# A gated delta net layer on one core: the order of instructions from a list instead of a list scheduler

## The chip, the cores and the metric

The kernel runs on one core of one Trainium2 chip. The metric is the device time of one launch in microseconds (us), and the kernel before takes 2705.01 us, the median of three runs (2702.5 to 2705.7). A core has TensorE (PE, matrix products), VectorE (DVE), ScalarE (ACT), GpSimd (POOL) and SyncE (SP, which issues transfers here). Each engine runs its own instructions in the order in which the program gives them, and waits on semaphores for the results of others.

## The reference, cut to what matters

One layer on 2048 tokens of width 1024: eight heads of a gated delta net (a linear attention with a state per head, in chunks) beside four heads of attention to a memory of 256 rows, an output projection, a layer norm, a squared-ReLU MLP of width 4096 and a second layer norm.

```python
proj = x @ w_in                                   # q, k, v, z, a, b and the memory queries
qkv = silu(causal_depthwise_conv(qkv, conv_w));  q, k = l2_normalize(q), l2_normalize(k)
beta = sigmoid(b);  g = -exp(a_log) * softplus(a + dt_bias)
# per chunk: A = I + strict_lower(beta k k^T * decay);  u, w = A^-1 (beta v), A^-1 (beta k e^g)
def step(state, inp):
    v_new = u_c - w_c @ state
    o = qd @ state + a_c @ v_new
    return state * dc + kd^T @ v_new, o
o = rms_norm(o, gate_norm_w) * silu(z)
m = memory_attention(mq, mem_k, mem_v)            # softmax over layer_norm(mem) @ w_mem_kv
x = layer_norm(ALPHA * x + concat(o, m) @ w_out, ln1_g, ln1_b)
x = layer_norm(ALPHA * x + square(relu(x @ w_ff1)) @ w_ff2, ln2_g, ln2_b)
```

## The kernel before, in words

Everything is float32. A large product is made of three passes of 128x512: each operand is split into a high part (a cast on ACT, `CAST whl<-wraw`, `CAST T<-xj`) and a low part (a subtraction on DVE), and `mm3` adds high x high, high x low and low x high. The tokens are worked in four blocks of 512.

*The mixer* goes through a block head by head. `dense` projects q, k and v (banks `aq`, `ak`, `av`), convolves them (`ck`, `cq`, `cv` are the results) and transposes them (`ptk`, `ptq`); `gate` projects z (`az`). `gdn_a` builds the matrix of a chunk (`pkq`), inverts it by a chain of small products with copies between them (`pq`, then `pp`, several times; the last copies, such as `Y<-pp` on ACT, write the inverse) and transposes v (`ptv`). `gdn_b` runs the recurrence (`pc`, `po`) and transposes the output (`pto`). The memory heads stand between (`amq`, `sps`, `pmT`, `pmo`); `memory_rows` makes the memory's keys and values ready once, beginning with sixteen transposes `pt<-ident,ym`, whose results ACT takes from the banks as `st`.

*The output projection* (`out_seven`, banks `ao`) and the two products of the MLP (`fA`, `fB`, `fC` and `f2A`, `f2B`, `f2C`) work on a pair of blocks by seven products in place of eight, with sums of operands kept in device memory. At the end of an output projection ACT normalises rows (`ACTIVATE y<-y,nb,rs`), PE transposes them (`pt<-ident,y`), ACT writes them out of the banks (`st<-pt,lnc`) and casts them (`CAST T<-st`), while the last of the seven products still runs; its weights come as `whl` (`CAST whl<-whl`).

*The start* (`first_tokens`): ten matmuls of ones (`warm`, two passes each), then the first 24 passes of `aq`, for which x comes in eight pieces (`xj`), with the sixteen products for a and b (`aab`) and a small transpose (`pln`) among them.

*What sets the order.* The code between the first constants and the end isn't issued as it is written. A `Recorder` keeps each operation with its reads and writes, and `issue` gives them all out at the end, so that all of them have one line in the profile, L447. In the kernel before, `issue` is a list scheduler: for each engine it keeps what is ready, takes what has the lowest priority number (an operation's index, plus `rec.shift`, plus an offset from the table `PLACE` of some 200 numbers that `spot` selects by stage), and adds up times by a table of costs (`cost`, `LAT`, `MARGIN`, `DRAIN`). It also models the number of buffers of a tag, so that no operation is given out before it has a place. `rec.gate` and `rec.join` hold transfers and matmuls behind others in this scheduler only. The program that results is run as usual: each engine in the order given, with the waits that reads and writes need.

Of the kernel before, what the change touches and what calls it, by code (L numbers as in the profile page):

```python
# [14 lines left out]
P = 128  # L15
# [14 lines left out]

LAT = {("PE", "PE"): 0, ("DVE", "POOL"): 190, ("ACT", "POOL"): 215, ("PE", "POOL"): 350, ("DVE", "DVE"): 130, ("ACT", "ACT"): 155, ("POOL", "POOL"): 100}
LAT_FROM = {"PE": 200, "DVE": 130, "ACT": 135, "POOL": 75, "SP": 60}
MARGIN, TURN = {"PE": 100, "DVE": 100, "ACT": 100, "POOL": 400, "SP": 100}, 40
DRAIN, SWITCH = {"DVE": 90, "ACT": 100, "POOL": 98}, 0


# [7 lines left out]
class Buf:  # L46


    def __init__(self, pool, shape, dtype, tag, bufs, name):
        self.pool, self.shape, self.dtype, self.tag, self.bufs, self.name = pool, shape, dtype, tag, bufs, name  # L50
        self.ap = None
        self.psum = pool.name == "ps"
        self.users = 0
        self.end = 0
        self.held = False
        self.first = None
        self.log = []
# [8 lines left out]

# [118 lines left out]
class Op:  # L185
    __slots__ = ("i", "eng", "fn", "args", "kw", "dur", "extra", "succ", "npred", "ready", "start", "end", "load", "last",
                 "bufs", "turns", "prio", "quads", "cols", "late", "lhs")


PLACE = {  # L190
# [31 lines left out]
}  # L222


class Recorder:
    def __init__(self, nc, tc):
        self.nc, self.tc, self.ops, self.shift, self.gate, self.base, self.join = nc, tc, [], 0, None, 0, []
        self.tags = {}
        for attr, eng in (("vector", "DVE"), ("scalar", "ACT"), ("gpsimd", "POOL"), ("tensor", "PE"), ("sync", "SP")):
            setattr(self, attr, _Engine(self, getattr(nc, attr), eng))  # L230

    def buf(self, pool, shape, dtype, tag, bufs, name):
        b = Buf(pool, shape, dtype, tag, bufs, name)
        self.tags.setdefault((pool.name, tag), []).append(b)
# [6 lines left out]
    def add(self, eng, fn, name, args, kw):  # L241
        o = Op()
        o.i, o.eng, o.fn, o.args, o.kw = len(self.ops), eng, fn, args, kw
        o.succ, o.npred, o.ready, o.extra, o.turns = [], 0, 0, 0, set()
        o.prio = o.i + self.shift + self.base
# [8 lines left out]
        o.dur = self.cost(o, name, wr, rd, args, kw)  # L254

        o.quads = {("r" if v in rd else "w", v.buf.psum): v.p0 // 32 for v in wr + rd[::-1]}
# [21 lines left out]
        for i, q in turns.items():  # L278
            if i not in preds:
                preds[i] = q  # L280
                q.turns.add(o.i)
        for q in preds.values():
            q.succ.append(o)
        o.npred = len(preds)
        o.bufs = list({id(r.buf): r.buf for r in rd + wr}.values())
        for b in o.bufs:
            if b.first is None:
                b.first = o.i
            b.users += 1
# [891 lines left out]

# [751 lines left out]
```

## Time and profile before

| | |
|---|---|
| median of three runs (lowest, highest) | 2705.01 us (2702.5, 2705.7) |
| profiled execution, its time | 2702.34 us |
| its span in the trace | 2700.6 us |
| PE busy | 2685.2 us, 99% |
| DVE, ACT, POOL busy | 2087.0 (77%), 1624.8 (60%), 423.3 us (16%) |
| share of the chain that ended last | PE 96%, DVE 2%, ACT 1% |
| transfers | 613.79 MB, 227 GB/s in the mean |

Busy time is the share of an engine's span in which the profile has an instruction on it. The ends of matmuls are modelled, and a matmul's recorded end lies behind the start of the next; distances between starts are the better measure of PE. The chain is followed back from the last instruction, at each step to what released it. In the timeline, a row is a run of instructions of one form: its start, the time from the first's start to the last's end, the engine, and behind `x` how many; in brackets the idle time before it and what ended it.

### The profile page before, as it was taken

The page shows a single profiled execution, that of the slowest core. Times are in us where ns is not written, and L with a number is a line of the kernel's source. Part 1 is how long each engine was busy: PE and PEld are TensorE (multiplying, and loading weights), DVE is VectorE, ACT ScalarE, POOL GpSimd, SP SyncE. Part 2 cuts the span into 40 slices and gives each one's busy share as a digit, 9 for nine tenths or more (in the row PEclk, how much of TensorE's full clock was granted, in tenths as well). Part 3 has the DMA queues.
Part 4 walks back from the last instruction along what each step waited for, and adds up shares of the span by engine and source line. Part 5 has one row for each costly group of instructions (what it writes and reads, how often), then busy time and mean ns, then how long its engine had stood idle before and what let it go on. Part 6 is the DMA issues. An engine that isn't in the chain of part 4 may idle for free.

```text
span 2700.6 us, 42393 instructions
## 1 busy us (share of the span) xinstructions
PE 2685.2 (99%) x13577; PEld 2248.5 (83%) x13577; DVE 2087.0 (77%) x5604; ACT 1624.8 (60%) x4098; POOL 423.3 (16%) x1023
## 2 busy tenths in 40 slices
PE   9999999999999999999999999999999999999998
PEld 7888888888888888888888888888887888888887
DVE  7998889998867776756778888789977656667575
ACT  7778777776575555334446776578756655544341
POOL 3333133331000000000032221233201000000001
PEclk9999999999999999999999999999999999999999
DMA  8676659868788888765664444444678644586673
GB/s 317 235 258 207 234 178 311 300 233 285 276 307 289 293 302 287 270 215 189 234 222 157 151 150 175 175 162 138 238 271 290 206 138 153 171 293 216 215 237 114
DMA packets 209070, 613.79 MB, mean 227 GB/s; under 512 B 24112, under 2 KB 32720, under 8 KB 188880
## 3 DMA queue, kind: packets, MB, share of 16 engines
q1 hardware_dynamic: 208416, 611.04, 65.0%
q8 instruction: 107, 1.75, 0.3%
q14 instruction: 115, 0.94, 0.1%
q10 hardware_dynamic: 432, 0.05, 0.0%
HBM read 436.35 MB, written 174.65 MB: 226 GB/s over the span
## 4 chain that ended last, share of the span: by engine, by line
PE 96%; DVE 2%; ACT 1%; DMA 0%; issue 0%; POOL 0%; POOLq 0%; ACTq 0%; DVEq 0%
PE f2A L447 13%; PE fA L447 13%; PE ao L447 8%; PE az L447 7%; PE fC L447 6%; PE f2C L447 6%; PE av L447 6%; PE ak L447 6%; PE aq L447 6%; PE fB L447 3%; PE f2B L447 3%; PE amq L447 3%; PE pc L447 3%; PE po L447 2%; PE pkq L447 2%; PE pq L447 1%
## 5 line engine op out<-in xcount | busy, mean ns | idle before, releaser
L447 DVE TENSOR_TENSOR whl<-wraw,whl 128x512 fp32r<-128x512 f32 (+2 forms) x294 | 256.9, 884 | 102.6 <-ACT whl L447 99.9
L447 ACT CAST whl<-wraw 128x512 fp32r<-128x512 f32 (+2 forms) x294 | 226.2, 780 | 182.6 <-PE fC L447 73.5
L447 PE MATMUL fA<-B,whl 128*128 128x512 f32 x1152 | 286.4, 389 | 0.0
L447 PE MATMUL f2A<-whl,X 128*128 128x512 f32 x1152 | 263.1, 389 | 0.0
L447 ACT CAST X<-X 128x1024 fp32r<-128x1024 f32 x118 | 124.1, 1052 | 228.1 <-DMA X<-xsc 174.6
L447 PEld LDWEIGHTS fA<-B,whl 128*128 128x128 f32 x1152 | 216.2, 188 | 45.0
L447 PEld LDWEIGHTS f2A<-whl,X 128*128 128x128 f32 x1152 | 216.3, 188 | 44.9
L447 DVE TENSOR_TENSOR X<-X,X 128x1024 fp32r<-128x1024 f32 x118 | 143.8, 1221 | 130.2 <-ACT X L447 130.0
L447 PE MATMUL az<-T,whl 128*128 128x512 f32 x768 | 215.9, 406 | 0.0
L447 PE MATMUL ak<-T,whl 128*128 128x512 f32 x768 | 213.4, 405 | 0.6 <-ACT cq L447 0.5
L447 PE MATMUL aq<-T,whl 128*128 128x512 f32 x768 | 210.6, 404 | 0.5 <-DVE T L447 0.4
L447 PE MATMUL av<-T,whl 128*128 128x512 f32 x768 | 209.3, 403 | 0.0
L447 PE MATMUL fC<-B,whl 128*128 128x512 f32 x768 | 196.9, 389 | 0.0
L447 PE MATMUL f2C<-whl,X 128*128 128x512 f32 x768 | 174.7, 389 | 0.0
L447 PEld LDWEIGHTS fC<-B,whl 128*128 128x128 f32 x768 | 144.1, 188 | 30.1 <-DVE B L447 0.2
L447 PEld LDWEIGHTS f2C<-whl,X 128*128 128x128 f32 x768 | 144.2, 188 | 29.9
L447 POOL TENSOR_SCALAR ve<-mv 128x1 f32<-128x1 f32 x34 | 15.6, 460 | 915.0 <-DVE mv L447 915.0
L447 PEld LDWEIGHTS aq<-T,whl 128*128 128x128 f32 x768 | 136.7, 189 | 25.3 <-DVE T L447 2.3
L447 PEld LDWEIGHTS ak<-T,whl 128*128 128x128 f32 x768 | 137.1, 189 | 24.3 <-ACT cq L447 0.6
L447 PEld LDWEIGHTS av<-T,whl 128*128 128x128 f32 x768 | 137.4, 189 | 23.2
L447 PEld LDWEIGHTS az<-T,whl 128*128 128x128 f32 x768 | 136.5, 189 | 22.4
L447 PE MATMUL ao<-whl,X 128*128 128x512 f32 x528 | 139.7, 403 | 0.0
(296 smaller groups left out, 6260.8 us busy)
## 6 DMA issues: line engine op xcount, KB each, us to landing
whl<-wsc SPq DMA_DIRECT2D x108, 1024.0 KB, 4.9
wraw<-in_w_ff_dram SPq DMA_DIRECT2D x106, 512.0 KB, 4.3
X<-xsc SPq DMA_DIRECT2D x96, 512.0 KB, 3.9
wsc<-whl SPq DMA_DIRECT2D x36, 1024.0 KB, 6.0
whl<-tsc SPq DMA_DIRECT2D x64, 512.0 KB, 4.8
xsc<-hB SPq DMA_DIRECT2D x96, 256.0 KB, 3.1
xo<-cat SPq DMA_DIRECT2D x80, 256.0 KB, 3.3
wraw<-in_w_in_dram SPq DMA_DIRECT2D x35, 512.0 KB, 5.9
```

The source lines that it names most:

```text
L447: o.fn(*[res(a) for a in o.args], **{k: res(v) for k, v in o.kw.items()})
```

## The change

The scheduler goes, with its costs, its offsets (`PLACE`, `spot`), shifts, gates and model of buffers. In its place stands a constant `ORDER`, a compressed and encoded string of some 260 lines, of which `order` makes the list of indices, each as the difference from the one before. `issue` takes the recorded operations in that order; it asserts that each comes behind those it depends on. The operations themselves, 23,656 of them, and their tiles are the same. In the profile their line is then L544.

```diff
-LAT = {("PE", "PE"): 0, ("DVE", "POOL"): 190, ("ACT", "POOL"): 215, ("PE", "POOL"): 350, ...}
-MARGIN, TURN = {"PE": 100, "DVE": 100, "ACT": 100, "POOL": 400, "SP": 100}, 40
...
-PLACE = {
-    ('w',): 140, (0, 0, 'D'): 5, (0, 0, 'F'): -5, (0, 0, 'H'): -585, (0, 1, 'D'): -70, (0, 1, 'F'): 75,
...
+    __slots__ = ("i", "eng", "fn", "args", "kw", "preds")
+ORDER = (
+    "c-rlKiIOC_j@%DLnDIXT|Hnjk2N;a3tezfeCGFa-&3j#0m6>rcNDy#19C2Rpy36`!*6W_@N8*q5$Jnp<@n5;xdUw6GzL49M`Esl`626eGQTVZY"
...
+def order():
+    import base64
+    import zlib
+
+    i = 0
+    for d in zlib.decompress(base64.b85decode(ORDER)).decode().split(","):
+        i += int(d)
+        yield i
...
-        o.prio = o.i + self.shift + self.base
...
-        if eng == "SP" and self.gate is not None:
-            preds[self.gate.i] = self.gate
-        if eng == "PE":
-            preds.update((q.i, q) for q in self.join)
...
+        o.preds = preds.keys() | turns.keys()
         self.ops.append(o)
...
     def issue(self):
-        import heapq
...
-            o = heapq.heappop(avail[e])[2]
...
-        out.sort(key=lambda o: (o.start, o.i))
+        out = [self.ops[i] for i in order()]
+        assert len({o.i for o in out}) == len(out) == len(self.ops)
+        done = set()
+        for o in out:
+            assert o.preds <= done, o.i
+            done.add(o.i)
         res = lambda v: v.get() if isinstance(v, Ref) else v
         with self.tc.manual_schedule():
             for o in out:
                 o.fn(*[res(a) for a in o.args], **{k: res(v) for k, v in o.kw.items()})
...
-    def spot(*key):
-        rec.base = PLACE.get(key, 0)
...
     def gate_rows(a, xs, ks):
-        rec.join = [q for x in xs for q, w, *_ in x.buf.log if w and q.eng == "SP"]
-        rec.shift -= 9999
```

Of PE's 12,495 recorded instructions 3,400 leave their relative order, of DVE's 5,089 1,862, of ACT's 3,648 1,468, of POOL's 1,014 485 and of SP's 1,410 482. PE's are moved by at most 214 places, in the median of those moved by 2. Three places follow.

PE at the start of the program, before; `warm` is the product of ones, `aq` the first projection, and the numbers behind `T` only tell tiles apart:

```order
L447 MATMUL warm<-ones 128x128 x10
L447 MATMUL aq<-T_157,whl 128x512
L447 MATMUL aq<-T_162,whl 128x512
L447 MATMUL aq<-T_157,whl 128x512 x2
L447 MATMUL aq<-T_162,whl 128x512
L447 MATMUL aq<-T_157,whl 128x512
L447 MATMUL aq<-T_176,whl 128x512
```

And in the list:

```order
L544 MATMUL aq<-T_104,whl 128x512
L544 MATMUL aq<-T_112,whl 128x512
L544 MATMUL warm<-ones 128x128 x10
L544 MATMUL aq<-T_104,whl 128x512 x2
L544 MATMUL aq<-T_112,whl 128x512
L544 MATMUL aq<-T_104,whl 128x512
L544 MATMUL aq<-T_138,whl 128x512
```

The products of ones, first before, now stand behind two passes of `aq`. On SP, the first transfer is now `xj` (before, a piece of `wraw`, then two of `xj`).

PE where the memory's rows are transposed, in the first block, before:

```order
L447 MATMUL az<-T_222,whl 128x512
L447 MATMUL az<-T_217,whl 128x512
L447 MATMUL pt<-ident,ym 128x128 x4
L447 MATMUL ptq<-ident,cq 128x128 x4
L447 MATMUL pt<-ident,ym 128x128 x12
L447 MATMUL aq<-T_157,whl 128x512
L447 MATMUL aq<-T_162,whl 128x512
```

And in the list, the first eight and, behind the `az`, the next:

```order
L544 MATMUL av<-T_202,whl 128x512
L544 MATMUL pkq<-kq 128x256
L544 MATMUL pt<-ident,ym 128x128 x8
L544 MATMUL ptk<-ident,ck 128x128 x4
L544 MATMUL az<-T_104,whl 128x512
L544 MATMUL az<-T_112,whl 128x512
L544 MATMUL az<-T_104,whl 128x512 x2
L544 MATMUL az<-T_112,whl 128x512
```

The sixteen transposes, four and twelve before, now stand as eight and, after some thirty rows, as 1, 1 and 6.

ACT near the end of the second output projection, where `y`, `st`, `T` and `whl` are as told above; before:

```order
L447 ACTIVATE y<-y,nb,rs 128x512
L447 ACTIVATE st<-pt,lnc 128x256 x2
L447 ACTIVATE y<-y,nb,rs 128x512
L447 CAST T_24186<-st 128x2x256
L447 ACTIVATE y<-y,nb,rs 128x512 x2
L447 CAST whl<-whl 128x1024 x2
L447 ACTIVATE st<-pt,lnc 128x256 x2
L447 CAST T_24226<-st 128x2x256
```

And in the list:

```order
L544 ACTIVATE y<-y,nb,rs 128x512
L544 CAST xh<-xl 128x512 x2
L544 ACTIVATE y<-y,nb,rs 128x512 x3
L544 ACTIVATE st<-pt,lnc 128x256 x2
L544 CAST whl<-whl 128x1024
L544 ACTIVATE st<-pt,lnc 128x256 x2
L544 CAST whl<-whl 128x1024
L544 CAST T_24204<-st 128x2x256
L544 CAST T_24206<-st 128x2x256
```

The four `y` stand in one piece of one and one of three, and the two casts of `whl`, together behind the last `y` before, now stand apart, each behind a pair of `st`. On PE, eleven transposes `pt<-ident,y` stood in one row there with `ao` behind them; now eight stand together, then 23 rows of `ao`, then nine. The last 14 rows of PE and of DVE in the program are the same in both.

## Rows read from the trace of the kernel before

**Rows 1.** The page, busy us, share of the span and instructions of each engine.

```profile
PE 2685.2 (99%) x13577; PEld 2248.5 (83%) x13577; DVE 2087.0 (77%) x5604; ACT 1624.8 (60%) x4098; POOL 423.3 (16%) x1023
```

**Rows 2.** The page, the chain that ended last, shares of the span.

```profile
PE 96%; DVE 2%; ACT 1%; DMA 0%; issue 0%; POOL 0%; POOLq 0%; ACTq 0%; DVEq 0%
```

**Rows 3.** Table of waits, PE: us in total, times, longest us.

```profile
PE ao L447 <- ACT whl L447: 1.4, 4, 0.6
...
PE pt L447 <- ACT st L447: 1.1, 1, 1.1
```

**Rows 4.** Busy us by stretch (PE, PEld, DVE, ACT, POOL), PEclk, DMA share, GB/s.

```profile
1.20:3.00 1.80, 1.80 (x8) 1.80 (x9) 0.56 (x2) 0.80 (x1) 1.76 (x7) 1.00 0.52 151
1146.00:1189.00 43.00, 43.00 (x191) 35.64 (x190) 26.46 (x29) 16.86 (x16) 2.10 (x4) 1.00 0.61 198
```

**Rows 5.** PE's timeline, end of the second output projection: start, us, line, operation.

```profile
2060.58 0.71 PE L447 MATMUL pt<-ident,y 128*128 128x128 f32 x5
2062.17 0.55 PE L447 MATMUL pt<-ident,y 128*128 128x128 f32 x3 [0.88 <-ACT y L447]
2062.88 0.55 PE L447 MATMUL pt<-ident,y 128*128 128x128 f32 x3 [0.16 <-ACT y L447]
2063.81 0.73 PE L447 MATMUL ao<-whl,xh 128*128 128x512 f32 x2 [0.39 <-ACT whl L447]
2064.76 0.96 PE L447 MATMUL ao<-whl,xh 128*128 128x512 f32 x3 [0.22 <-ACT whl L447]
```

**Rows 6.** ACT's timeline at the same place.

```profile
2062.72 1.99 ACT L447 CAST whl<-whl 128x1024 fp32r<-128x1024 f32 x2
```

**Rows 7.** PE's timeline, end of the first output projection.

```profile
733.20 0.27 PE L447 MATMUL pt<-ident,y 128*128 128x128 f32 x1
734.09 0.73 PE L447 MATMUL ao<-whl,xh 128*128 128x512 f32 x2 [0.62 <-ACT whl L447]
735.05 0.97 PE L447 MATMUL ao<-whl,xh 128*128 128x512 f32 x3 [0.22 <-ACT whl L447]
```

**Rows 8.** PE's timeline, the memory's rows.

```profile
53.02 0.82 PE L447 MATMUL pt<-ident,ym 128*128 128x128 f32 x6
54.95 0.66 PE L447 MATMUL pt<-ident,ym 128*128 128x128 f32 x4 [1.11 <-ACT st L447]
```

**Rows 9.** PE's timeline, `ak` behind `cq`.

```profile
507.81 1.88 PE L447 MATMUL ak<-T,whl 128*128 128x512 f32 x7 [0.49 <-ACT cq L447]
```

**Rows 10.** PE's timeline, small waits: the first, one of the largest, the last.

```profile
62.75 0.98 PE L447 MATMUL pkq<-kq 128*128 128x256 f32 x6
...
407.97 1.78 PE L447 MATMUL av<-T,whl 128*128 128x512 f32 x7
410.02 0.66 PE L447 MATMUL ptv<-ident,cv 128*128 128x128 f32 x4 [0.26 <-ACT Y L447]
...
1914.48 0.39 PE L447 MATMUL pc<-R,Y 128*128 128x128 f32 x2
```

**Rows 11.** PE's timeline, the start.

```profile
1.19 4.57 PE L447 MATMUL warm<-ones 128*128 128x128 f32 x20 [1.19 <-POOL mhalf L534]
5.48 0.51 PE L447 MATMUL aq<-T,whl 128*128 128x512 f32 x1
...
11.92 1.92 PE L447 MATMUL aab<-xj,abw 128*32 128x512 f32 x16
...
15.48 0.74 PE L447 MATMUL ak<-T,whl 128*128 128x512 f32 x2
```

**Rows 12.** SP's issues, the start.

```profile
0.79 0.39 SPq L447 DMA_DIRECT2D wraw<-in_w_in_dram  x1
1.24 0.90 SPq L447 DMA_DIRECT2D xj<-in_xt_dram  x2
```

**Rows 13.** ACT's timeline, the start.

```profile
4.79 0.62 ACT L447 CAST T<-xj 128x512 fp32r<-128x512 f32 x1 [0.80 <-DMA xj<-in_xt_dram]
```

**Rows 14.** PE's timeline, the last matmul.

```profile
2691.78 0.39 PE L447 MATMUL f2A<-whl,xl 128*128 128x512 f32 x1
```

More of the change, by code (lines that the diff above doesn't have):

```diff
@@ L27 @@
 QO, KO, VO, ZO, AO, MO = 0, 1024, 2048, 3072, 4096, 4112
-LAT = {("PE", "PE"): 0, ("DVE", "POOL"): 190, ("ACT", "POOL"): 215, ("PE", "POOL"): 350, ("DVE", "DVE"): 130, ("ACT", "ACT"): 155, ("POOL", "POOL"): 100}
-LAT_FROM = {"PE": 200, "DVE": 130, "ACT": 135, "POOL": 75, "SP": 60}
-MARGIN, TURN = {"PE": 100, "DVE": 100, "ACT": 100, "POOL": 400, "SP": 100}, 40
-DRAIN, SWITCH = {"DVE": 90, "ACT": 100, "POOL": 98}, 0
 def _prod(v):
@@ L52, in __init__ @@
         self.psum = pool.name == "ps"
[L53 to L56, printed above, removed]
         self.log = []
@@ L253, in add @@
         rd = [v for v in rd if isinstance(v, Ref)]
-        o.dur = self.cost(o, name, wr, rd, args, kw)
-        o.quads = {("r" if v in rd else "w", v.buf.psum): v.p0 // 32 for v in wr + rd[::-1]}
         preds, turns = {}, {}
@@ L336, in issue @@
-    def issue(self):
-        import heapq
-        engs = ("PE", "DVE", "ACT", "POOL", "SP")
-        free = {e: 0.0 for e in engs}
-        soon = {e: [] for e in engs}
-        avail = {e: [] for e in engs}
-        dma = [0.0]
-        quads, cols = {e: {} for e in DRAIN}, P
-        slots = {k: [0.0] * v[0].bufs for k, v in self.tags.items()}
-        order = {k: sorted((b for b in v if b.users), key=lambda b: b.first) for k, v in self.tags.items()}
-        pos = {}
-        for k, v in order.items():
-            for i, b in enumerate(v):
-                b.key = k
-        head = {k: 0 for k in order}
-        wait = {k: [] for k in order}
-        def ahead(b):
-            v, h = order[b.key], head[b.key]
-            while h < len(v) and v[h].held:
-                h += 1
-            head[b.key] = h
-            c = 0
-            while v[h] is not b:
-                c += not v[h].held
-                h += 1
-            return c
-        def place(o):
-            for b in o.bufs:
-                if not b.held:
-                    if len(slots[b.key]) <= ahead(b):
-                        wait[b.key].append(o)
-                        return
-                    b.held = True
-                    b.since = heapq.heappop(slots[b.key])
-                    again(b.key)
-                o.ready = max(o.ready, b.since)
-            heapq.heappush(soon[o.eng], (o.ready, o.i, o))
-        def again(k):
-            if wait[k]:
-                w, wait[k] = sorted(set(wait[k]), key=lambda q: q.i), []
-                for q in w:
-                    pending.append(q)
-        pending = [o for o in self.ops if o.npred == 0]
-        out = []
-        fed = 0.0
-        while True:
-            while pending:
-                place(pending.pop(0))
-            best = None
-            for e in engs:
-                if avail[e]:
-                    t = free[e]
-                elif soon[e]:
-                    t = max(free[e], soon[e][0][0])
-                else:
-                    continue
-                if best is None or t < best[0]:
-                    best = (t, e)
-            if best is None:
-                break
-            t, e = best
-            while soon[e] and soon[e][0][0] <= t:
-                r, i, o = heapq.heappop(soon[e])
-                heapq.heappush(avail[e], (o.prio, i, o))
-            o = heapq.heappop(avail[e])[2]
-            if e == "PE":
-                if o.cols != cols:
-                    t += SWITCH
-                    cols = o.cols
-                t = max(t, fed + o.load)
-                fed = t + o.dur - o.last
-            if e in DRAIN:
-                at = quads[e]
-                if any(at.get(k, q) != q for k, q in o.quads.items()):
-                    t = max(t, free[e] + DRAIN[e])
-                at.update(o.quads)
-            o.start, o.end = t, t + o.dur
-            free[e] = o.end
-            if o.extra:
-                dma[0] = max(o.end + 1700, dma[0]) + o.extra - 1700
-                o.end = dma[0] + o.late
-            out.append(o)
-            for s in o.succ:
-                lat = LAT.get((e, s.eng), LAT_FROM[e])
-                if e == "PE" and lat and o.last < 60:
-                    lat += 65 if o.last > 30 else 130
-                if lat:
-                    lat += MARGIN[e] + (s.load if s.eng == "PE" and s.lhs in o.bufs else 0)
-                s.ready = max(s.ready, o.end + (TURN if s.i in o.turns else lat))
-                s.npred -= 1
-                if s.npred == 0:
-                    pending.append(s)
-            for b in o.bufs:
-                b.users -= 1
-                b.end = max(b.end, o.end)
-                if b.users == 0:
-                    heapq.heappush(slots[b.key], b.end + LAT_FROM[e] + 100)
-                    again(b.key)
-        left = [o for o in self.ops if o.npred or not hasattr(o, "start")]
-        assert len(out) == len(self.ops), (len(out), len(self.ops))
-        out.sort(key=lambda o: (o.start, o.i))
-        self.total = max(o.end for o in out)
@@ L1220, in hybrid_layer @@
     xo, Xd = {}, {}
-    LATE = (7, 11)
     def keep_out_sums(u, j):
@@ L1553, in wpart @@
             return load_rows(w_ff2, u + HU * (n[1] == "2"), int(n[2]) - 1)
-        banks, pe_op = {}, [None, None]
+        banks = {}
         tags = {"A": ("ga0", "ga1", "pb", "pb"), "B": ("acc", "acc", "acc", "m")}
@@ L1566, in part @@
                 if u not in xs:
-                    if last:
-                        rec.gate = pe_op[1]
                     xs[u] = xpart(xn, u, last)
-                    rec.gate = None
                     ws[u] = wpart(wn, u)
@@ L1584, in ff2 @@
                     affine(*((ln2_g, "kq0"), (ln2_b, "kq1"))[u - 2])
-                rec.gate = None
                 for t in range(NC):
                     part(u, t)
-                    pe_op[0] = rec.ops[-1]
-                    if n == 5 and u == 1:
-                        pe_op[1] = rec.ops[-1]
                     if u == HU - 1:
@@ L1757, in weights @@
             return load_rows(w_out, OU[int(name[1]) - 1][u], int(name[2]) - 1)
-        banks, xs, ws, held = {}, {}, {}, {}
+        banks, xs, ws = {}, {}, {}
         at = {"A": ("acc", "acc", "acc", "m"), "C": ("pb", "pb", "ga0", "ga1")}
@@ L1764, in part @@
             if (n, u) not in xs:
-                rec.gate = held.get(GATE.get(n))
-                spot(s, n, u, "X")
                 xs[n, u] = operand(n, xn, u)
-                spot(s, n, u, "W")
                 ws[n, u] = weights(wn, u)
-                spot(None)
-                rec.gate = None
             x, w = xs[n, u], ws[n, u]
```

402 lines of the change are left out of this document (301 added, 101 removed), and 30 rows, old and new, of the table PLACE.

## The prediction

> **What bounds the kernel now.** I read the page first. TensorE (PE) is busy for 99% of the span [rows 1], and the chain that ended last lies on PE for 96% of it, with 2% on VectorE (DVE) and 1% on ScalarE (ACT) [rows 2]. So a new order can win only where PE stands still, and can lose only by making it stand still. The profile puts matmul ends by a model, so I next took the spacing of starts. In a stretch with nothing but 128x512 passes, 191 of them start in 43.00 us, 0.225 us each, 0.227 by single rows; this is the price of a long pass [rows 4]. A short one (a transpose or a 128x128 pass) costs 0.11: five take 0.71 and one takes 0.27, so four steps take 0.44 [rows 5, 7]. Then I walked PE's timeline and took, from each distance between starts, the work that stands in it. What is left over is waiting. It comes in four places and a tail of small ones.
>
> First, the end of the second out projection. From 2060.58 to 2064.76 us there are 4.18 us with eleven transposes and two long passes in them, 11 x 0.11 + 2 x 0.227 = 1.66, so 2.5 us are waits, on ACT's `y` and `whl` [rows 5]. ACT normalises rows (`y`) there and then casts two weight tiles, 1.99 us, which PE waits for [rows 6]. Second, the end of the first out projection: 733.20 to 735.05 is 1.85 us with 0.11 + 0.45 of work, so 1.3 us [rows 7]; the table of waits names the same releaser, `whl`, and beside it `st` [rows 3]. Third, the memory rows: 53.02 to 54.95 is 1.93 us with six transposes, 0.66, so 1.3 us, on `st` [rows 8]. Fourth, `ak` behind `cq`, 0.5 us [rows 9]. The small ones are 32 places, the first at 62.75 and the last at 1914.48, together 4.1 us by the same subtraction; the one at 410.02 is among the largest: 407.97 plus seven long passes is 409.56, so 0.46 us [rows 10]. That is 9.7 us in all outside the start, and it bounds the gain.
>
> **The change, part by part.** The 23,656 recorded operations are the same in both kernels, with the same tiles; no work goes and none comes. Scheduler, offsets and due times are host code and cost nothing on the chip. So every term is a wait that goes, comes or stays.
>
> *End of the second out projection.* Before, eleven transposes stand in one row on PE, each pair waiting for its `y`, and the long passes behind them wait for `whl`, which ACT casts only after the last `y`. In the list, eight transposes are followed by 23 rows of `ao`, 33 long passes or 7.5 us, before the next nine, and on ACT the `y` operations come in a block of three while a cast of `whl` stands between two pairs of `st`. Either way PE has long passes while ACT works. I take all 2.5 us as gone; the other end is none gone, if the eight now meet the same late `y`. Nearer to all, since 7.5 us of cover stands against a wait of 2.5.
>
> *End of the first out projection.* The same function and the same kind of wait, 1.3 us; taken as gone, other end none. Together with the former: -3.8.
>
> *Memory rows.* Before, twelve transposes follow each other and the last four wait for `st`, whose operations on ACT alternate with others. Now eight stand at one place and the other eight, in pieces of 1, 1 and 6, behind `az`, `pkq` and `aq`. The piece of six can still be short of a bank. Of 1.3 I take 0.9; ends 0 and 1.3.
>
> *`ak` behind `cq`.* In the list, `ak` now follows two `pq` instead of two `pq`, two `aq`, three `pto`, `pc`, `pto` and two `pp`, and the neighbours have changed on ACT too. Half or so: -0.3 of 0.5; ends 0 and 0.5.
>
> *Small waits.* 3,400 of PE's 12,495 instructions leave their relative order, by at most 214 places. Some of the 32 small waits get more cover, and other places less. Ends: all 4.1 gone, or 4.1 still there in other places. I take -1.5, nearer to nothing, because a wait that goes has a neighbour that comes closer to its own limit.
>
> *Start.* Here the list costs something. Before, ten `warm` matmuls (20 passes) fill PE from 1.19 to 5.48 us, until the first `x` has landed and been cast [rows 11]. In the list two `aq` come first, and `warm` stands behind them. PE stays idle until the first `aq`; SP now issues `xj` first, at 0.79 instead of 1.24 us [rows 12], and the cast of it that began at 4.79 and took 0.62 [rows 13] begins up to 0.45 earlier, so the first `aq` starts at 5.0 to 5.5, say 5.3. Two `aq` at twice 0.227 make 0.9. Then `warm`: 20 passes took 4.29 us before (0.214 each), and at 0.11 each would take 2.2; it ends at 8.4 to 10.5. Sixteen `aq` follow. The eighteen of before needed 5.48 to 11.92, 0.36 each, since `x` was still coming; now data has had `warm` as cover, so 16 x 0.227 = 3.6 up to 16 x 0.36 = 5.7. Then `aab`, `pln` and six `aq` as before, 11.92 to 15.48, 3.56. The first `ak` comes at 15.6 to 19.8 instead of 15.48, +0.1 to +4.3. I take +1.5, in the lower half, because the data that the sixteen wait for has landed when `warm` is through.
>
> [...]
>
> *SP and the other queues.* SP's issues move too (482 of 1,410), POOL's 485 of 1,014, DVE's 1,862 of 5,089 and ACT's 1,468 of 3,648. I cost these at nothing: PE's long passes hide them, and where the cover is gone the price is that of a small wait, below. *The end.* The last 14 rows of PE and DVE are the same, so the 8.4 us from the last matmul, which ends at 2692.17 [rows 14], to 2700.6 stay.
>
> **Sum.** -2.5 - 1.3 - 0.9 - 0.3 - 1.5 + 1.5 = -5.0 us. The profiled execution took 2702.34 us (span 2700.6 and 1.7 around it), so this one would take 2697.3. The median of the runs, 2705.01, is 2.7 above the profiled one; the forecast is 2705.0 - 5.0 = 2700.0.
>
> **The rivals.**
> *A, the forecast*, 2700.0, 0.56; its own range 2697 to 2703.
> *B, waits only change places.* The terms go, and as many come elsewhere, because the same accumulator banks and the same ACT serve the same work: 2705. For it: so many instructions moved by so little. Against it: the four places have one cause each, and the list breaks each up. 0.13.
> *C, slower by the inversion chain.* In each of 32 heads `ptv` needs a bank that ACT's copy `Y<-pp` sets free; where too few PE instructions stand between the last `pp` and `ptv`, PE waits, as at 410.02, 0.46 us [rows 10]. In the lists, at most five instructions stand between in one head before and in 13 now; at most six in 14 before and in 21 now. If all of the 32 pay 0.46, that is 14.7 us: 2705.0 - 5.0 + 14.7 = 2714.7. It eats the gain from 11 heads on (5.0 / 0.46) and is slower than can be told from no change from 23 heads on, at 2710.6. Against it: of the 14 close heads only that one paid as much. 0.10.
> *D, all waits go.* 5.6 at the four places and 4.1 small, with the start at +0.1 to +1.5: -9.6 to -8.2, so 2695.4 to 2696.8. For it: PE never lacks work, only order. 0.17.
> *E, the start stays at the slow pace.* If all 22 `aq` up to the first `ak` ran at twice 0.227, 22 x 0.227 = 5.0 us on top: 2705. For it: the first passes' spacing [rows 11]. Against it: PE would be running for several us by then, and before, it was at pace before 15.48. [...] 0.04.
> That the program runs another order than the list cannot well be: it issues the list itself.
>
> **Numbers.** About 0.2%, 5.4 us, is what a measurement of this kernel can tell from no change: faster means below 2699.6, slower above 2710.4. A lies below 2699.6 with 0.27 of its 0.56, and D with all its 0.17: faster 0.44. Same is the rest of A, B and E, less what falls outside: 0.43. Slower is C and 0.03 from B's and E's upper ends: 0.13. The range: all waits gone and the start at +0.1 gives 2695.4, less the 3.2 us by which the three runs differ, 2692; no wait gone and the start at +4.3 gives 2709.3, so 2709.
>
> **What would show it.** In the profile of the changed kernel: PE's timeline without gaps over 0.3 us around 2060 to 2066 and 730 to 737; `st` and `y` gone from, or small in, the table of waits; `warm` between 6 and 11 us and the first `ak` at 16 to 18 us; the same 8.4 us after the last matmul. Wrong would be: `ptv` or `pp` in the table of waits with a count of ten or more; `ao` still waiting for `whl`; or a start beyond 19 us.

## The result: 0.19% slower

| | before | list |
|---|---|---|
| median of 15 runs each | 2703.62 us | 2708.35 us |
| lowest, highest | 2702.33, 2705.7 | 2707.02, 2711.8 |
| profiled execution, its time | 2702.34 us | 2709.15 us |
| its span | 2700.6 us | 2707.4 us |

The ratio is 1.0019, with a 95% interval of 1.0012 to 1.0026: 4.7 us slower, where 5.0 us faster was forecast. That is inside the 5.4 us of "same", and clear of zero in fifteen runs. The profiled executions are 6.8 us apart, since that of before lies 1.3 us under its median and that of the list 0.8 us above.

The page of the list first, busy time by engine and the chain that ended last; the rows of before are [rows 1, 2].

```profile
PE 2684.3 (99%) x13577; PEld 2250.0 (83%) x13577; DVE 2101.2 (78%) x5604; ACT 1626.2 (60%) x4098; POOL 425.2 (16%) x1023
...
PE 93%; DVE 3%; DMA 1%; ACT 1%; POOL 1%; issue 0%; SPq 0%; POOLq 0%; DVEq 0%; ACTq 0%
```

PE's busy time is the same within a us, and the chain has lost 3% on PE to DVE, POOL and transfers. PE's work takes no longer (DVE's busy time is 14 us more); PE stands still more. The table of waits, PE (us in total, times, longest), says for whom:

```profile
PE aq L544 <- ACT whl L544: 5.5, 1, 5.5
PE fA L544 <- DVE B L544: 1.9, 1, 1.9
PE pp L544 <- ACT inv L544: 1.3, 4, 0.6
PE pkq L544 <- DVE Xc L544: 1.0, 1, 1.0
PE pto L544 <- ACT on L544: 0.9, 1, 0.9
PE ptv L544 <- ACT Y L544: 0.8, 2, 0.5
...
PE pq L544 <- ACT inv L544: 0.5, 1, 0.5
```

The `st` and `whl` of [rows 3] and the `y` of [rows 5] are gone, and so is `ak` behind `cq`. In their place stand one wait at the start (5.5 us, where before `warm` ran), one of `fA`, and a crowd in the inversion and the recurrence (`pp`, `pq`, `pkq`, `ptv`, `pto`).

Where the time went is seen best by equal work: comparing when PE, in either trace, has the same amount of passes behind it. This is how much later PE is in the list (the passes taken at their prices, 0.227 and 0.11, the starts as they are):

| time in the list | what has just ended | later by | change |
|---|---|---|---|
| 33.5 us | start | 2.0 us | +2.0 |
| 58.7 us | memory's rows | 0.6 us | -1.4 |
| 129 us | `ak` to `az` of the first heads | 0.4 us | -0.2 |
| 684 us | mixers of the first two blocks | 8.1 us | +7.7 |
| 795 us | end of the first out projection | 6.6 us | -1.5 |
| 1364 us | MLP of the first pair | 6.5 us | -0.1 |
| 2060 us | mixers of the second pair | 7.5 us | +1.0 |
| 2091 us | end of the second out projection | 4.9 us | -2.6 |
| 2123 us | first products of the second MLP | 7.0 us | +2.1 |
| 2699 us | last matmul | 7.0 us | 0.0 |

The three named waits went as forecast. The end of the second out projection, PE's timeline of the list, answers to [rows 5]: transposes in fours and threes between long passes, no bracket.

```profile
2064.28 0.60 PE L544 MATMUL pt<-ident,y 128*128 128x128 f32 x4
2064.63 0.71 PE L544 MATMUL ao<-whl,xh 128*128 128x512 f32 x2
...
2065.64 0.49 PE L544 MATMUL pt<-ident,y 128*128 128x128 f32 x3
```

The start answers to [rows 11 to 13]. PE's timeline, then ACT's and SP's:

```profile
5.46 1.22 PE L544 MATMUL aq<-T,whl 128*128 128x512 f32 x2 [5.46 <-ACT whl L544]
6.48 3.56 PE L544 MATMUL warm<-ones 128*128 128x128 f32 x20
9.80 3.92 PE L544 MATMUL aq<-T,whl 128*128 128x512 f32 x16
...
17.53 0.50 PE L544 MATMUL ak<-T,whl 128*128 128x512 f32 x1
```

```profile
8.97 0.41 ACT L544 CAST whl<-wraw 128x256 fp32r<-128x256 f32 x1 [0.72 <-DMA wraw<-in_w_in_dram]
```

```profile
5.51 0.91 SPq L544 DMA_DIRECT2D wraw<-in_w_in_dram  x2
```

PE stands still until 5.46, and the second piece of `wraw`, which SP issues only at 5.51 (behind four `xj` and `alog`), is cast at 8.97. The first `ak` starts at 17.53, 2.05 us later than in [rows 11].

The wait that I had not foreseen, `fA`. PE's timeline, then DVE's and SP's issues:

```profile
2109.28 1.52 PE L544 MATMUL fA<-B,whl 128*128 128x512 f32 x6
2112.70 1.43 PE L544 MATMUL fA<-B,whl 128*128 128x512 f32 x5 [1.91 <-DVE B L544]
```

```profile
2108.10 0.69 DVE L544 TENSOR_TENSOR t<-e,b 128x512 f32<-128x512 f32 x1
2110.75 0.69 DVE L544 TENSOR_TENSOR B<-b,B 128x512 fp32r<-128x512 f32 x1 [1.96 <-DMA x1d<-y]
2111.36 0.69 DVE L544 TENSOR_TENSOR b<-b,t 128x512 f32<-128x512 f32 x1
2111.96 1.29 DVE L544 TENSOR_TENSOR B<-t,B 128x512 fp32r<-128x512 f32 x2
```

```profile
2100.63 1.82 SPq L544 DMA_DIRECT2D x1d<-y  x2
```

DVE forms operands of `fA` in its order. The low part at 2110.75 goes to a place that still holds a row of `y`; the store of that row, `x1d<-y`, is issued at 2100.63 and has landed only when DVE goes on, 10.0 us after its issue. How much of that is the late issue and how much the slow store was not separated. The operand that `fA` needs stands two behind it.

And one of the crowd, `pkq` at 466.80, which waited 1.13 us. POOL's timeline, then PE's:

```profile
455.18 0.26 POOL L544 TENSOR_SCALAR ss<-ss 128x8 f32<-128x8 f32 x1 [9.54 <-ACT jq L544]
...
463.68 0.63 POOL L544 COPY raw<-halo 128x3 f32<-128x3 f32 x1 [7.64 <-DVE Bc L544]
464.28 1.03 POOL L544 TENSOR_TENSOR rk<-ss,mhalf 128x4 f32<-128x4 f32 x1
...
465.67 0.20 POOL L544 TENSOR_TENSOR bh<-bh,rk 128x4 f32<-128x4 f32 x1
```

```profile
465.45 0.40 PE L544 MATMUL ak<-T,whl 128*128 128x512 f32 x1
466.80 0.83 PE L544 MATMUL pkq<-kq 128*128 128x256 f32 x5 [0.96 <-DVE Xc L544]
```

`ss` is ready at 455.4. `rk`, which needs only `ss`, stands on POOL behind `raw<-halo`, which waits until 463.68 for DVE to free its place. `bh` follows `rk`, DVE's `dl` follows `bh`, and the bank that `pkq` needs comes free after that. One operation stands in front of another in a queue: 8.8 us of delay, 1.1 us of it seen by PE (by the starts: 465.45 plus one long pass is 465.68, and `pkq` starts at 466.80).

### The profile page after: what moved, and what is told of

The parts are those of the page before. It is cut to its first block, busy times and chain, and to the rows that moved or that the text cites. A ratio compares the mean times of both kernels' runs of the same rounds, so it can differ in the third digit from the quotient of the medians.

```text
span 2707.4 us, 42339 instructions
## 1 busy us (share of the span) xinstructions
PE 2684.3 (99%) x13577; PEld 2250.0 (83%) x13577; DVE 2101.2 (78%) x5604; ACT 1626.2 (60%) x4098; POOL 425.2 (16%) x1023
## 4 chain that ended last, share of the span: by engine, by line
PE 93%; DVE 3%; DMA 1%; ACT 1%; POOL 1%; issue 0%; SPq 0%; POOLq 0%; DVEq 0%; ACTq 0%
PE f2A L544 13%; PE fA L544 13%; PE ao L544 8%; PE f2C L544 6%; PE fC L544 6%; PE ak L544 6%; PE az L544 6%; PE aq L544 6%; PE av L544 6%; PE f2B L544 3%; PE fB L544 3%; PE pc L544 3%; PE amq L544 3%; PE po L544 2%; PE pkq L544 2%; PE pp L544 1%
## 5 line engine op out<-in xcount | busy, mean ns | idle before, releaser
L544 DVE TENSOR_TENSOR whl<-wraw,whl 128x512 fp32r<-128x512 f32 (+2 forms) x294 | 257.2, 886 | 113.7 <-ACT whl L544 111.6
L544 ACT CAST whl<-wraw 128x512 fp32r<-128x512 f32 (+2 forms) x294 | 225.3, 778 | 189.2 <-PE fC L544 55.4
L544 PE MATMUL fA<-B,whl 128*128 128x512 f32 x1152 | 286.9, 389 | 1.9 <-DVE B L544 1.9
L544 PE MATMUL f2A<-whl,X 128*128 128x512 f32 x1152 | 263.2, 389 | 0.0
L544 ACT CAST X<-X 128x1024 fp32r<-128x1024 f32 x118 | 123.8, 1051 | 222.6 <-DMA X<-xsc 168.3
L544 PEld LDWEIGHTS fA<-B,whl 128*128 128x128 f32 x1152 | 216.1, 188 | 47.2 <-DVE B L544 2.3
L544 PEld LDWEIGHTS f2A<-whl,X 128*128 128x128 f32 x1152 | 216.3, 188 | 44.9
L544 DVE TENSOR_TENSOR X<-X,X 128x1024 fp32r<-128x1024 f32 x118 | 143.9, 1221 | 119.6 <-ACT X L544 119.5
L544 PE MATMUL aq<-T,whl 128*128 128x512 f32 x768 | 219.7, 403 | 5.5 <-ACT whl L544 5.5
L544 PE MATMUL az<-T,whl 128*128 128x512 f32 x768 | 221.7, 404 | 0.0
L544 PE MATMUL av<-T,whl 128*128 128x512 f32 x768 | 220.0, 403 | 0.0
L544 PE MATMUL ak<-T,whl 128*128 128x512 f32 x768 | 218.9, 402 | 0.0
L544 PE MATMUL fC<-B,whl 128*128 128x512 f32 x768 | 197.6, 389 | 0.0
L544 PE MATMUL f2C<-whl,X 128*128 128x512 f32 x768 | 175.4, 389 | 0.0
L544 PEld LDWEIGHTS fC<-B,whl 128*128 128x128 f32 x768 | 144.2, 188 | 30.0
L544 PEld LDWEIGHTS f2C<-whl,X 128*128 128x128 f32 x768 | 144.2, 188 | 29.9
L544 POOL TENSOR_SCALAR ve<-mv 128x1 f32<-128x1 f32 x34 | 17.9, 528 | 955.2 <-DVE mv L544 952.8
L544 PEld LDWEIGHTS aq<-T,whl 128*128 128x128 f32 x768 | 138.9, 189 | 29.3 <-ACT whl L544 5.5
L544 PEld LDWEIGHTS ak<-T,whl 128*128 128x128 f32 x768 | 139.1, 189 | 23.8 <-ACT whl L544 0.4
L544 PEld LDWEIGHTS az<-T,whl 128*128 128x128 f32 x768 | 138.2, 189 | 24.2 <-issue 1.7
L544 PEld LDWEIGHTS av<-T,whl 128*128 128x128 f32 x768 | 138.8, 189 | 23.0
L544 PE MATMUL ao<-whl,X 128*128 128x512 f32 x528 | 143.9, 403 | 0.8 <-DVE X L544 0.5
```

The lines of the kernel that those rows point to most:

```text
L544: o.fn(*[res(a) for a in o.args], **{k: res(v) for k, v in o.kw.items()})
```

## The experiments

Two theories were stated first. L: the list loses by single displaced operations, each worth its own wait, and a wait removed is time won. The rival: in the mixers PE's suppliers have no time to give, and a wait removed comes back at the next place. All times below are medians, with the ratio to the kernel before, which has 2703.5 in the same rounds; the list's 2708.35 is from the rounds of the result. What a wait is said to be worth is taken from distances between starts, and is a little more than the idle time in the brackets.

**warm_first.** The ten products of ones go to the front of PE's order.

```diff
 PE
+MATMUL warm<-ones 128x128 x10
 MATMUL aq<-T_104,whl 128x512
 MATMUL aq<-T_112,whl 128x512
-MATMUL warm<-ones 128x128 x10
```

> The list, with the ten warm matmuls at the very front of PE's order and nothing else moved. Theory L (the new order loses by single displaced operations, each worth its own wait): PE has its 20 first passes done before x lands, as before, the first ak comes about 2.0 us earlier than the list's 17.53, and the whole takes 2.0 us less than the list, 2706.3. Rival (the start is set by the landing of x, and warm only fills the time): the sixteen aq then wait for x instead, first ak within 0.5 us of 17.53, no gain.

2710.28 us, ratio to before 1.0022 (1.0013 to 1.0031): nothing gained, and the rival holds. PE's timeline shows why: `warm` hid in the wait for the loads, and the first `ak` comes only 0.4 us earlier.

```profile
1.19 4.25 PE L534 MATMUL warm<-ones 128*128 128x128 f32 x20 [1.19 <-POOL mhalf L621]
...
9.80 3.40 PE L534 MATMUL aq<-T,whl 128*128 128x512 f32 x12 [1.99 <-ACT whl L534]
...
17.16 0.44 PE L534 MATMUL ak<-T,whl 128*128 128x512 f32 x1
```

That it is slower than the list comes from elsewhere. By equal work this trace loses 2.8 us more than the list's at `fA`: the waits there are 3.2 us instead of 2.1, and behind them PE's passes run at half pace, which costs another 1.6. PE's timeline, then the busy times by stretch, where the third number from the end is the granted clock:

```profile
2113.31 1.72 PE L534 MATMUL fA<-B,whl 128*128 128x512 f32 x5 [2.26 <-DVE B L534]
```

```profile
2114.34:2117.75 3.41, 3.41 (x9) 2.64 (x8) 3.41 (x7) 2.60 (x5) 0.00 (x0) 0.50 0.11 48
```

From 2114.39 to 2117.38 the long passes start 0.427 us apart instead of 0.227, at a granted clock of 0.50, after PE had waited 2.4 us. The traces of patched and list_light show the same at `fA`, and that of start_before both there and at the memory's rows; those of the list, fa_fix, sup_fix and sup_more do not. So a difference of 1 to 2 us between two of these runs needs the trace beside it.

**start_before.** Everything up to 46 us as before, the loads too.

```diff
-out = LIST
+out = BEFORE up to az at 46 us, then LIST without what has been issued
```

> The list, with everything up to 46 us in the order of the kernel before, the loads on SP too. Theory (the start is set by the order of the loads, for with warm alone in front aq waited 2.0 us for whl, whose load SP issues at 5.5 us instead of 2.2): the 2.0 us of the start come back, 2706.3. Rival (the start's loss is caught up later, since PE then waits for ACT and DVE anyway): the list's time within 0.7 us.

2711.24 us, 1.0030 (1.0018 to 1.0041), slower still, though the start itself did come back. By equal work PE is 0.4 us behind before at 32 us instead of 2.0. With warm_first, where `warm` alone changed nothing, this fits the order of the loads as what sets the start, though the orders of all engines came back here. But then the memory's transposes wait, which they don't in the list:

```profile
57.25 0.38 PE L536 MATMUL pt<-ident,ym 128*128 128x128 f32 x2
59.95 0.66 PE L536 MATMUL pt<-ident,ym 128*128 128x128 f32 x4 [2.32 <-ACT st L536]
```

Behind that wait PE runs at half pace, at a granted clock of 0.50, from 61.06 to 64.47 us. Here the list's gain at the memory's rows came only together with the list's start. What in the start it hangs on I did not settle: the joint (the place where one order passes into the other) itself displaces some 40 operations. The traced execution took 2716.19 us, 5 us over the median; against the list's trace it loses 2.8 us at `fA` and 2.6 in the first MLP, where the order is the list's.

**mixer1_before.** The order before between 100 and 700 us.

```diff
-out = LIST
+out = LIST up to av at 100 us, BEFORE up to ao at 700 us, then LIST
```

> The list up to about 100 us and from about 700 us on; in between (the mixer of the first two blocks) the operations in the order of the kernel before. Theory L: the 7.4 us that the list loses there by the two traces (from +0.8 to +8.1 us against the kernel before) come back, so about 7 us less than the list, 2701, and 2 to 3 us less than the kernel before. Rival (the loss there comes from what the other stages leave behind: transfers and buffers, or it is one slow execution's): at most 2 us come back, 2706 or more.

2704.04 us, 1.0001 (0.9993 to 1.0010): 4.3 us back by the medians, 6.1 by the profiled executions. In the stretch itself all came back: 0.3 us ahead of before at 108 us and 0.5 ahead at 676, where the list loses 7.4. The loss lies in the order of that stage. Behind it `ao` now waits 1.2 us at the joint, and `fA` twice, 2.6 us in all.

**patched.** 22 groups on PE, each of which waited over 0.15 us, go behind the 1 to 5 long passes that followed; two operations each on DVE and ACT go back with them.

```diff
 PE (one of 22, pkq at 466.80)
-MATMUL pkq<-kq 128x256 x5
 MATMUL ak<-T,whl 128x512 x2
 ...
+MATMUL pkq<-kq 128x256 x5
```

> The list, with 22 short groups of PE (pto, pp, pq, pkq, ptv and po of the mixers, each of which waited 0.2 to 1.1 us, 10.3 us in all) put behind the 1 to 5 long passes that followed them. Theory L (each wait is a local lack of long passes in front): most of the 10.3 us go, 2699 to 2702. Rival (ACT, DVE and POOL are the bound in the mixers, so that PE has to wait somewhere): the waits come back at the next groups, within 2.5 us of the list, 2706 or more.

2708.65 us, 1.0018 (1.0009 to 1.0027): by the medians none of 10.3 us won. By equal work the mixers of the first two blocks lose 7.2 us as against 7.4, those of the second pair 1.1 less than in the list, and the half pace at `fA` takes 1.6 back in the traced execution. Theory L falls in this form. PE's timeline shows the waits at the next short group; the first stood at `pto`, 139.52 us, and the second is a new one:

```profile
138.29 0.64 PE L534 MATMUL av<-T,whl 128*128 128x512 f32 x2
139.69 0.63 PE L534 MATMUL pq<-YP,inv 128*128 128x64 f32 x4 [0.76 <-POOL e L534]
```

```profile
525.61 0.94 PE L534 MATMUL av<-T,whl 128*128 128x512 f32 x3
527.80 0.55 PE L534 MATMUL ptv<-ident,cv 128*128 128x128 f32 x3 [1.24 <-ACT Y L534]
```

Where PE no longer waited for one supplier here, it was only earlier at the next thing that a supplier was late with (0.76 us at `pq`, 1.24 at `ptv`).

**pe_of_before.** PE alone takes the order before in that stage.

```diff
-PE, DVE, ACT, POOL, SP: LIST
+PE between 100 and 700 us: BEFORE; the others: LIST, displaced where that must be
```

> The list, with PE's instructions between 100 and 700 us in the order of the kernel before; of the other engines 220 operations are displaced as little as that needs, against 1,593 that differ between the two orders there. Theory P (in the first mixers the list lets PE run ahead of its suppliers): about 7 us come back, 2701 to 2703. Rival S (the list's order on ACT, DVE and POOL is what makes the results late, and PE's order matters little): at most 2.5 us come back, 2706 or more, or it is slower than the list.

2798.09 us, 1.0350 (1.0336 to 1.0364): 90 us slower. Theory P, that PE's order alone was at fault, is dead. PE's order before does not go with the list's order on the other engines. PE's table of waits has the same kinds, many times over:

```profile
PE pto L531 <- ACT on L531: 14.9, 9, 3.5
PE ptv L531 <- ACT Y L531: 6.8, 6, 2.3
PE pc L531 <- DVE state L531: 6.6, 3, 4.8
```

Not all of the 90 us are waits. By starts, waits over 0.15 us come to some 70 us from 100 to 700 us, as against 9.4 in the list; some 10 us more are passes at half pace, for the granted clock falls to 0.50 eight times in that stage. The busy times by stretch where it is lowest, 0.90 in the mean, with PE busy for 82 of 100 us:

```profile
500.00:600.00 100.00, 82.03 (x411) 67.11 (x409) 75.22 (x264) 53.95 (x171) 22.45 (x63) 0.90 0.69 239
```

The reverse, PE of the list with the others of before, was not tried.

**sup_fix.** The suppliers: `raw<-halo` on POOL and one cast of `whl` on ACT, with its low part on DVE, go behind the operations that stood behind them.

```diff
 POOL
-COPY raw<-halo 128x3
 TENSOR_TENSOR rk<-ss,mhalf 128x4
 TENSOR_TENSOR bh<-beta,rk 128x4
 TENSOR_TENSOR bh<-bh,rk 128x4
+COPY raw<-halo 128x3
 ACT
-CAST whl<-wraw 128x1024
 ACTIVATE dl / COPY inv x4 / ACTIVATE inv x2
+CAST whl<-wraw 128x1024
```

> The list, with two operations moved that stood in front of a queue and waited: on POOL a copy raw<-halo that waits for DVE, moved behind rk and bh, which stood 8.8 us behind it (pkq then waited 1.13 us at 466.8); on ACT a cast of whl that waits for a load, moved with its low part behind the eight copies of the inversion that follow (pp waited 0.78 and 0.22 us at 169 to 173). Theory S (a result is late since its operation stands behind another one that waits, and the wait goes when it doesn't): both waits go and stay gone, about 2.1 us less than the list, 2706.3. Rival (the engines are full, and the waits come back at the next group): the same as the list within 0.8 us.

2707.98 us, 1.0016 (1.0007 to 1.0024): 0.4 us by the medians, the rival's result, but by two opposite parts. On POOL `rk` ran at 456.9, and `pkq`'s 1.13 us went and stayed gone. On ACT the wait went from `pp` (0.8 us) and came back twice as long at the following `pq`. PE's timeline, first where `pkq` had waited, then `pq`:

```profile
466.53 0.76 PE L534 MATMUL pkq<-kq 128*128 128x256 f32 x5
```

```profile
169.97 1.09 PE L534 MATMUL aq<-T,whl 128*128 128x512 f32 x4
172.57 0.44 PE L534 MATMUL pq<-inv 128*72 128x64 f32 x4 [1.51 <-DVE inv L534]
```

**sup_more.** As sup_fix's POOL part and fa_fix, and ten long DVE operations behind the short copies that they held up.

```diff
 DVE (one of ten, 368 us)
-SCALAR_TENSOR_TENSOR ck<-raw,cw,ck 128x512
 TENSOR_SCALAR Y<-pp
+SCALAR_TENSOR_TENSOR ck<-raw,cw,ck 128x512
```

> The list with twelve operations moved, none on PE: the operand of fA as in fa_fix, the copy raw<-halo on POOL as in sup_fix, and ten 512-wide operations on DVE (ck, cq, cv, cat, mq) that stood or ran in front of a short copy of the inversion, each put behind it; PE waited for those copies 0.25 to 0.69 us in eight places, 3.4 us in all, beside 1.13 for the POOL place and 2.07 for fA. Theory S (PE waits because short operations of the inversion's chain queue behind long ones that nobody waits for): 4 to 6 us come back, 2702 to 2704. Rival (the engines are full in the mixers, a wait removed comes back at the next place): what fa_fix gave and no more, 2706 to 2707.

2706.90 us, 1.0014 (1.0005 to 1.0023): what fa_fix gives and no more, the rival. The trace tells the places apart. `ptv` at 368 us (0.69) and at 446 (0.25) and `pkq` at 467 (1.13) went and stayed gone. The waits at 488, 524 and 561 us (0.48, 0.29, 0.63) became 1.00, 0.85 and 0.87, and in the second pair 0.73 at 1879 to 1880 and 0.35 at 1917 became 0.74 and 0.89. The busy times (PE, PEld, DVE, ACT, POOL) of the list suggest what separates them; DVE is third:

```profile
320.00:380.00 60.00, 59.02 (x337) 50.14 (x336) 51.39 (x198) 43.22 (x154) 20.73 (x46) 1.00 0.51 177
440.00:500.00 60.00, 58.63 (x325) 48.83 (x323) 55.50 (x211) 44.88 (x150) 17.86 (x47) 1.00 0.82 282
560.00:620.00 60.00, 59.38 (x370) 52.02 (x369) 57.28 (x222) 49.86 (x173) 17.03 (x41) 1.00 0.72 255
```

From 320 to 380 us DVE is busy for 51.4 of 60, in the two later stretches for 55.5 and 57.3. My reading is that where DVE has time to spare, a short copy can go first, and where it has 5 to 8% left, the long operation that steps back is itself late for somebody. That is argued, not shown: `ptv` at 446 stayed gone and the wait at 488 came back, in the same stretch.

**list_light.** The list with 24 subtractions on DVE left out.

```diff
             for o in out:
+                if o.i in SKIP:       # 24 subtractions of keep_out_sums
+                    continue
                 o.fn(...)
```

> The list without 24 DVE subtractions of 0.69 us each in the second block's mixer (those that form the sums of the out projection's weights; the sums are stored without them), 16.5 us of DVE's 54 to 57 busy us in each 60 there. Theory S or the rival of full engines: with DVE's queue shorter, more than half of PE's waits over 0.1 us between 320 and 680 us go (6.2 us in the list), and the time falls by 3 us or more. Other rival (the waits are latency of the chain itself, from engine to engine, or loads): they stay, 5 us or more of them, and the time falls by less than 1.5 us.

2706.52 us, 1.0011 (1.0003 to 1.0020): 1.8 us less than the list, between the two answers. The waits over 0.15 us from 320 to 700 us fall from 12 and 6.1 us to 7 and 3.5. DVE's queue is nearly half of it there; `pkq` at 466 (POOL's queue) stays at 1.14 and `pq` at 559 at 0.6, and a `pp` at 366 waits 0.6 where in the list the `ptv` behind it did. The traced execution took 2708.98 us, 2.5 over the median, and 1.7 us of it go to half pace at `fA`.

**fa_fix.** One operation on DVE.

```diff
 DVE
-TENSOR_TENSOR B<-b,B 128x512      # waits for the store of x1d
 TENSOR_TENSOR b<-b,t 128x512
 TENSOR_TENSOR B<-t,B 128x512      # what fA needs
+TENSOR_TENSOR B<-b,B 128x512
```

> The list, with one DVE operation moved: the low part of an operand of fA that waits for a store of x1d (it stood in front of the one that the first fA needs, and held it for 2.0 us) goes behind that one. Theory: the 2.07 us wait of fA at 2112.7 goes, so 2.1 us less than the list, 2706.3. Rival (the DVE and ACT work for the operands is late altogether): fA waits for the next operand instead, the same as the list within 0.7 us.

2706.65 us, 1.0014 (1.0005 to 1.0023): 1.7 us less than the list, as the theory has it. `fA` still waits 0.8 us by starts, where the list has 2.1:

```profile
2109.73 2.20 PE L534 MATMUL fA<-B,whl 128*128 128x512 f32 x9
2112.53 0.73 PE L534 MATMUL fA<-B,whl 128*128 128x512 f32 x2 [0.61 <-DVE B L534]
```

**best_of_both.** The order before, with the list's three gaining stretches set in.

```diff
-out = LIST
+out = BEFORE to 46 us, LIST to 100, BEFORE to 700, LIST to 900,
+      BEFORE to 2031, LIST to 2088, BEFORE to the end
```

> The kernel before's order up to 46 us, the list's for the memory rows (46 to 100 us), the order before through the first mixers (to 700 us), the list's for the end of the first out projection (700 to 900), the order before up to 2031 us, the list's for the end of the second out projection (2031 to 2088), and the order before from there. Theory L (each stage keeps the gain or loss that it showed in the two traces): -1.3, -1.4 and -2.6 us against the kernel before and none of the losses, 2703.6 - 5.3 = 2698.3. Rival (a gain at the end of an out projection is given back right behind it, since fA then waits for its operands, as it did for 1.6 us with the first mixers in the order before): one or both of the last two go, 2701 to 2703.

2705.50 us, 1.0008 (0.9999 to 1.0016), beyond even the rival: 2 us above before. The gains do not travel. At the memory's rows `st` holds PE 2.3 us, at the first out projection -1.3 us is met by +1.4 at the joint, and behind the second one -2.0 is followed by +2.6:

```profile
2094.41 0.66 PE L585 MATMUL pt<-ident,y 128*128 128x128 f32 x4 [0.65 <-ACT b L585]
...
2097.99 1.67 PE L585 MATMUL fC<-B,whl 128*128 128x512 f32 x6 [0.87 <-ACT b L585]
```

**mixers_before.** The list, but the order before in the mixers of both pairs, and fa_fix.

```diff
-out = LIST
+out = LIST to 100 us, BEFORE to 700, LIST to 1250, BEFORE to 2031, LIST to the end
+      fA's operand moved as in fa_fix
```

> The list at the start and in the memory rows, at the ends of the out projections and in the MLP, the order of the kernel before in the mixers of both pairs (100 to 700 and 1250 to 2031 us), and fA's operand moved as in fa_fix. Theory (what the list loses on balance it loses in the mixers and at fA; the rest of it is worth a little): mixer1_before's 2704.0 less 0.9 for the second pair's mixers and less 1.7 for fA, 2701.4, 2 us under the kernel before. Rival (the waits at the seams and at fA come back whatever stands there): 2703.5 or more.

2701.06 us, 0.9990 (0.9981 to 0.9998): faster than both kernels, 2.4 us under before and 7.3 under the list, and within 0.4 of what was expected. PE's waits, of which the first replaces `warm`, `ao` stands just behind a joint at 702.7 us, and `fA` at 2077.8 us:

```profile
PE aq L586 <- ACT whl L586: 5.2, 1, 5.2
PE fA L586 <- DVE T L586: 1.2, 1, 1.2
PE ao L586 <- DVE whl L586: 1.1, 1, 1.1
PE ak L586 <- ACT cq L586: 0.5, 1, 0.5
```

These two take back much of the list's gains: by equal work 0.2 of 1.5 us are left at the end of the first out projection and 1.3 of 2.6 at that of the second. At `fA` behind the second end nothing is lost. The traced executions are 1.3 us apart (2701.06 and 2702.34 us), less than the medians, since that of before lies under its median.

## Why the prediction was wrong

*The end of the second out projection*, -2.5 forecast: -2.6. *The end of the first*, -1.3: -1.5. *Memory's rows*, -0.9: -1.4. *`ak` behind `cq`*, -0.3: about -0.4, its wait is gone. *The start*, +1.5: +2.0, but by another mechanism. I took `warm` on PE's path for the price; warm_first shows that it hides in a wait for `whl`, which fits SP's new order of loads (the second piece issued at 5.51 instead of 2.18 us). The first `ak` is at 17.53, inside the forecast's 16 to 18, though with luck: the terms of that sum lie on a path that is not what binds.

The half-speed rival E had a part, but hardly a price. In the list the second `aq` takes 0.427 us, and the `warm` passes are 0.213 apart up to 8.83 us and 0.111 from 8.99 on; the sixteen `aq` behind them run at 0.225 to 0.236, but for the first and the last. Before, the `warm` passes were 0.213 apart throughout, but for the first two, 0.375 apart. In warm_first the pace doubles at 4.9 us already, and yet its first `ak` is only 0.4 us earlier, since PE then waits for `whl` until 9.80 and again, at 13.66, for a row of `lnr`. The 1.00 of the granted clock from 1.20 to 3.00 us in [rows 4] is no reading so early: the trace's record of the clock begins at 5.56 us in the kernel before, 8.93 in the list and 4.90 in warm_first, which in the last two is where the pace doubles. What sets the pace of the first passes, and what ends it, no run here shows.

*The end*: 8.2 us behind the last matmul, against 8.4.

*The small waits* are the step that failed: -1.5 forecast, between 0 and -4.1, and the mixers came to +7.7 and +1.0. I bounded the term by what could go and held, of what could come, only "4.1 still there". Before, waits over 0.15 us from 100 to 700 us were 8 with 2.6 us; in the list they are 18 with 9.4. Of these, 13 with 6.7 us lie in the inversion chain and its transposes (`pkq`, `pq`, `pp`, `ptv`), which is rival C's, at 0.10 in my chances; but only two, 0.95 us, are at `ptv`, the place that C priced, and its sign (`ptv` or `pp` ten times or more in the table of waits) did not come, for `pp` stands there with four and `ptv` with two. I had counted PE instructions between two steps, where the lateness sits in the suppliers' queues. From the two traces: in 416 steps of the chain (13 matmul groups in each of 32 heads), the time from the last result read to PE's start was under 0.2 us in 18 before and in 29 in the list, and 1 us or more in 52 before and in 122 in the list. So 346 steps had between 0.2 and 1 us in hand before, and 265 in the list. And the chain's operations, from having their data to starting, stood in POOL's queue 242 us in all before and 1667 in the list, in ACT's 524 and 891, in DVE's 1245 and 1609. Most of that costs nothing; 18 places cost 9.4 us.

*SP and the other queues*, which I costed at nothing ("PE's long passes hide them"), failed with it, and once more at *`fA`*, +2.1, which stood in no term: a store that SP issues at 2100.63 us, seen two operations later on DVE. I had asked what is late next behind each stall only on PE. Between the forecast of -5.0 and the +6.8 of the two traces lie 11.8 us; 10.5 of them are the mixers (-1.8 forecast with `ak`, +8.7 measured) and 2.1 `fA`.

What stays open: how much of the mixers' loss is DVE's queue and how much POOL's and ACT's. list_light puts DVE near half in the second block; for the first I have single places only. That the list's order in the mixers is what loses is shown (mixer1_before, mixers_before); that it loses by its suppliers' queues is shown at single places (`pkq` at 467, `fA`) and for the 24 subtractions. Why the memory's gain hangs on the list's start is not settled either.

## What to carry to other kernels

Where one engine is busy for 99% and the next, in the mixers, for up to 95%, an order is worth what its suppliers' queues are worth: read for every engine which operation stands behind one that waits, not how much work stands between two steps on the busy one. Here waits removed by moving PE's own work came back at the next short group; of those removed on a supplier some stayed away and some came back, perhaps by the time that the supplier has left. And gains of single stages in a list did not add up in another list: take a whole stage, and price the joint. A wait can also cost more than its length, if PE's clock falls behind it: in warm_first the waits at `fA` took 3.2 us, and the half pace behind them, at a granted clock of 0.50, cost another 1.6.

## What the runs showed of the hardware that I had not expected

Several waits of an order repeat almost to the tenth: `pto` at 139 us waits 1.05, 1.04, 1.04, 1.03 and 1.04 us in the list, warm_first, fa_fix, start_before and sup_fix, although PE arrives there up to 4 us apart, and `pkq` behind DVE's `Xc` 1.0 us in the tables of waits of the first four. Others don't, for the first mixers by equal work lose 7.4, 7.2, 6.3 and 5.8 us in the first four, with the same order there. A wait behind a store doesn't either: `fA` at 2107 to 2118 us lost 2.1, 3.2 and 3.2 us in the list, warm_first and start_before with the same order.

The granted clock of PE can fall for a few us in the middle of a kernel whose PE is busy for 99%. In four traces it reads 0.50 for 3.4 us behind a wait: 2.4 us in warm_first, 2.0 in patched, 2.4 in list_light, 2.5 and 2.4 in start_before; in pe_of_before it falls eight times from 100 to 700 us, for up to 10 us. It did not fall behind the list's 2.1 us at `fA`, nor behind 2.5 us at the memory's rows in best_of_both, so the length of the wait alone doesn't decide it here.
